# Layer 1's query, key and value projections as seven block products, with sums of the input streamed from DRAM

## The chip, the cores and the metric

The kernel runs on one core of a Trainium2 chip. The metric is the time of one execution on the device, in microseconds (us). A profile of one execution gives the records of TensorE (PE, with its weight loads as PEld), VectorE (DVE), ScalarE (ACT), GpSimd (POOL) and SyncE (SP, which issues the DMAs).

## The reference

The model is a two-layer encoder on 1024 tokens of width 1024, in float32. Layer 0 mixes tokens by neighbourhood attention, layer 1 by differential attention; each layer ends with a gated convolutional channel mixer and a gated embedding. The change touches layer 1's mixer only:

```python
def diff_attention(h, w_qkv, lam, subln_g, w_o, t5_table, lambda_init):
    q, k, v = jnp.split(h @ w_qkv, 3, axis=-1)      # 1024 x 3072
    # 8 heads; q and k of two 64-wide halves, q scaled by 1/8; v 128 wide
    ...
    def block_fn(args):                             # a block of 128 queries
        s = jnp.einsum('bhmqd,bhmkd->bhmqk', qb, k) + bias[None, :, None]
        a = jax.nn.softmax(s, axis=-1)
        w = a[:, :, 0] - lam_full * a[:, :, 1]
        return jnp.einsum('bhqk,bhkd->bhqd', w, v)
    ...
    o = rms_norm(o, subln_g) * (1.0 - lambda_init)
    return o @ w_o
```

`h` is the normalised input, `w_qkv` is 1024 x 3072, and the output o is 1024 x 1024.

## The kernel before

Every float32 operand of a projection is split into a high part, rounded by ACT to the type fp32r (`high`, L135), and a low part, the rest, by DVE (`low`, L138). A product is then three matmuls (`mm3`, L170): high by high, high by low, low by high. A block of 128 output columns by 512 tokens takes 8 slices of the inner width, so 24 matmuls of 128x512 into one PSUM bank; 128 columns by all 1024 tokens take 48. Layer 1's projections are 24 such column blocks: for each of 8 heads one of keys, one of queries, one of values, 1152 matmuls.

They run as a filler of the attention. `da` (L701) walks 64 steps n (8 heads of 8 query tiles). A step puts on PE, in this order, the values of tile n-1 (`da_values`, 8 matmuls), the scores of tile n+1 (`da_scores`, 12 matmuls), the first turn of tile n (`da_turn`, 4 transposes), some projection, the second turn, some projection, the small turn of tile n-1's output (`da_out`), and some projection. `tick` (L431) hands out the projection: it draws the generator `qkv_stream` (L323) forward, 6 draws of three matmuls in each step. `need` goes on drawing until the keys and queries, or the values, of a head are there. For each head the stream goes through keys, queries and values, with one weight block of 128 columns in use and the next being split. A finished bank of keys or queries is split into high and low on ACT and DVE; values are copied to SBUF, turned by PE and copied into `v` (L390).

Around a step, DVE adds the bias table T to the scores and takes a minimum (`softmax_pre`, L465), ACT takes the exponentials (L469), DVE combines the two softmaxes (L647 to L650), ACT and DVE copy the turned tile (L665, L667), ACT squares the values with a sum (L679), DVE adds a constant (L680), POOL takes the power -1/2 (`root`, L185), DVE scales the values (L682), and ACT copies their turn out (L698). T has one page for each head, loaded whole (L632).

The order on PE is the order of the program. A list scheduler sets the order on DVE, ACT, POOL and SP before the run; at run time each engine takes its instructions strictly in that order. Buffers come from rings of pages: `raw` holds three pages of 4 KB for each partition, `ws` four, `r1` and `r2` four larger ones each; projections have two PSUM banks (`pj`), turns and values two (`tr`), and scores the other four.

At the end of the stream come the embedding's product (`embeddings`, 96 matmuls), the output projection of the heads that are done (`first_out`), and the last head's (`second_out`).

## Time and profile before

| what | us |
|---|---|
| three runs | 2705.47, 2705.64 (median), 2705.91 |
| span of the profiled execution | 2703.4 |
| median of the runs less that span (the profiled execution's time is recorded as its span alone) | 2.2 |

By stage of the profiled execution (busy time of each engine, us; windows in us from the span's start):

| window | what runs | PE | DVE | ACT | POOL |
|---|---|---|---|---|---|
| 0 to 640 | layer 0, attention | 624.7 | 477.1 | 359.6 | 114.1 |
| 640 to 1010 | layer 0, channel mixer's first part | 368.9 | 278.9 | 154.8 | 114.1 |
| 1010 to 1285 | layer 0's end, layer 1's input | 275.0 | 191.5 | 132.8 | 21.7 |
| 1285 to 1330 | layer 1's first projections | 45.0 | 22.2 | 18.0 | 0.6 |
| 1330 to 1885 | layer 1's attention with its projections | 552.7 | 377.5 | 298.2 | 35.5 |
| 1885 to 2060 | the next stage | 172.9 | 141.2 | 87.0 | 21.8 |
| 2060 to 2703 | layer 1's rest | 636.6 | 449.8 | 269.8 | 129.8 |

The granted PE clock is 1.00 in all of these windows. An engine's busy time in a window is an upper bound of what it needs only where records do not overlap: PE's matmuls overlap, so their spacing is read from their starts. A row of the instructions in order of time gives start, duration, engine, line, operation, output<-inputs by the program's names and the shape; what stands in brackets at its end is how long the engine sat idle before it, and what ended that. A row of groups gives the count, the busy time and the mean in ns, and behind the second bar the idle time before the group with what ended it.

### The profile page before, as it was taken

The numbers are of one execution on the slowest core, as the hardware profiler recorded it, in microseconds if no ns is written. First come the engines' busy times: TensorE is split into PE (matmuls) and PEld (weight loads), VectorE is DVE, ScalarE is ACT, GpSimd is POOL, SyncE is SP. The second block draws the span as 40 slices with busy tenths as digits, with TensorE's granted clock in tenths as the row PEclk, the third lists the DMA queues.
The fourth block names the chain that finished last, engine by engine and source line by source line (L and its number), as shares of the span: only waits on it lengthen the run. The fifth ranks groups of instructions, "written<-read, shape, count | busy, mean of one in ns | idle before, by whom it ended". The sixth has DMA issues, their size and how long they took to land.

```text
span 2703.4 us, 36590 instructions
## 1 busy us (share of the span) xinstructions
PE 2675.6 (99%) x13492; PEld 2216.0 (82%) x13492; DVE 1938.2 (72%) x3334; ACT 1320.1 (49%) x2469; POOL 437.4 (16%) x445
## 2 busy tenths in 40 slices
PE   8999999999999999999999999999999999999999
PEld 6888887878888888888888888888878888888887
DVE  6777777699777767676566666676699777767674
ACT  5555556454344444454455555555454444444452
POOL 2221220003333300001000000000103334300000
PEclk9999999999999999999999999999999999999999
DMA  6213226423332373333211111123423232373442
GB/s 184 85 66 104 77 94 197 130 71 126 108 110 101 109 269 132 117 129 117 78 47 46 46 47 47 53 79 129 140 71 133 97 115 96 112 263 128 117 138 100
DMA packets 129334, 297.97 MB, mean 110 GB/s; under 512 B 11737, under 2 KB 37721, under 8 KB 129154
## 3 DMA queue, kind: packets, MB, share of 16 engines
q1 hardware_dynamic: 129154, 295.63, 33.1%
q8 instruction: 106, 1.74, 0.2%
q14 instruction: 74, 0.61, 0.1%
HBM read 221.17 MB, written 86.61 MB: 114 GB/s over the span
## 4 chain that ended last, share of the span: by engine, by line
PE 92%; DVE 4%; DMA 2%; ACT 2%; issue 1%; POOL 0%; SPq 0%; ACTq 0%; POOLq 0%; DVEq 0%
PE b L173 21%; PE b L174 21%; PE b L175 21%; PE g L830 6%; PE m L830 5%; PE b L676 4%; PE s L640 4%; PE b L662 2%; PE b L204 2%; PE b L830 2%; PE av L536 2%; PE b L509 1%; DMA x<-in_x 1%; PE s L490 1%; PE s L489 1%
## 5 line engine op out<-in xcount | busy, mean ns | idle before, releaser
L173 PE MATMUL b<-r,ws 128*128 128x512 f32 (+1 forms) x1344 | 547.0, 407 | 1.6 <-DVE r L308 1.6
L174 PE MATMUL b<-r,ws 128*128 128x512 f32 (+1 forms) x1344 | 519.6, 387 | 0.6 <-DVE r L139 0.4
L175 PE MATMUL b<-r,ws 128*128 128x512 f32 (+1 forms) x1344 | 519.1, 386 | 0.0
L175 PEld LDWEIGHTS b<-r,ws 128*128 128x128 f32 x1344 | 252.8, 188 | 53.1
L173 PEld LDWEIGHTS b<-r,ws 128*128 128x128 f32 x1344 | 253.4, 189 | 49.7 <-issue 3.3
L174 PEld LDWEIGHTS b<-r,ws 128*128 128x128 f32 x1344 | 254.2, 189 | 36.3 <-DVE r L139 1.9
L469 ACT ACTIVATE E<-E,mn 128x1024 f32<-128x1024 f32 (+2 forms) x256 | 221.5, 866 | 102.2 <-DVE mn L465 101.9
L173 PE MATMUL b<-r,r 128*128 128x512 f32 x680 | 268.8, 395 | 1.4 <-ACT ws L1571 1.0
L173 PE MATMUL b<-r,wa 128*128 128x512 f32 x688 | 268.0, 390 | 2.0 <-DVE B L1222 2.0
L175 PE MATMUL b<-r,wa 128*128 128x512 f32 x688 | 268.0, 389 | 0.0
L174 PE MATMUL b<-r,wa 128*128 128x512 f32 x688 | 267.7, 389 | 0.0
L174 PE MATMUL b<-r,r 128*128 128x512 f32 x680 | 265.2, 390 | 0.0
L175 PE MATMUL b<-r,r 128*128 128x512 f32 x680 | 265.0, 390 | 0.0
L185 POOL TENSOR_TENSOR ss<-ss,mhalf 128x1 f32<-128x1 f32 x128 | 74.9, 586 | 1093.5 <-DVE ss L680 560.2
L139 DVE TENSOR_TENSOR ws<-raw,ws 128x512 fp32r<-128x512 f32 (+3 forms) x168 | 167.8, 1005 | 53.4 <-ACT ws L136 51.9
L136 ACT ACTIVATE r<-raw 128x512 fp32r<-128x512 f32 (+1 forms) x168 | 110.6, 665 | 192.0 <-PE b L174 169.2
L136 ACT ACTIVATE ws<-raw 128x512 fp32r<-128x512 f32 (+3 forms) x168 | 124.5, 748 | 114.2 <-PE b L175 51.9
L139 DVE TENSOR_TENSOR r<-raw,r 128x512 fp32r<-128x512 f32 (+1 forms) x168 | 126.9, 760 | 68.4 <-ACT r L136 65.2
L830 PE MATMUL m<-r,ws 128*128 128x512 f32 x672 | 156.4, 391 | 0.0
L830 PE MATMUL g<-r,ws 128*128 128x512 f32 x672 | 155.8, 391 | 0.0
L465 DVE CUSTOM_DVE_ANT_0 E<-s,T 128x1024 f32<-128x1024 f32 x128 | 151.0, 1217 | 4.1 <-PE s L640 4.1
L173 PEld LDWEIGHTS b<-r,wa 128*128 128x128 f32 x688 | 129.2, 188 | 29.9 <-DVE B L1222 3.2
(188 smaller groups left out, 5072.5 us busy)
## 6 DMA issues: line engine op xcount, KB each, us to landing
raw<-in_w_in SPq DMA_DIRECT2D x86, 512.0 KB, 3.5
raw<-in_qkv SPq DMA_DIRECT2D x48, 512.0 KB, 5.6
spillS<-r SPq DMA_DIRECT2D x88, 256.0 KB, 3.0
r<-in_ffn_w_out SPq DMA_DIRECT2D x40, 512.0 KB, 6.0
raw<-spillS SPq DMA_DIRECT2D x40, 512.0 KB, 3.7
spillA<-B SPq DMA_DIRECT2D x66, 256.0 KB, 2.8
raw<-spillA SPq DMA_DIRECT2D x30, 512.0 KB, 3.9
x<-x SPq DMA_DIRECT2D x24, 512.0 KB, 3.6
```

The source lines that it names most:

```text
L136: return self.nc.scalar.activation(hi, src, AF.Copy).ins
L139: return self.nc.vector.tensor_tensor(out=lo, in0=src, in1=hi.bitcast(F32), op=ALU.subtract).ins
L173: mm(out, sta[0], mov[0], start=first, stop=False, skip_group_check=onto)
L174: mm(out, sta[0], mov[1], start=False, stop=False, skip_group_check=onto)
L175: mm(out, sta[1], mov[0], start=False, stop=last, skip_group_check=onto)
L185: self.nc.gpsimd.tensor_tensor(out=ss, in0=ss, in1=self.mhalf, op=ALU.pow)
L204: self.nc.tensor.transpose(t[:, k * P : k * P + P], h[:, c : c + P], self.ident)
L465: nc.vector.tensor_tensor_reduce(out=e, in0=s, in1=bias, scale=1.0, scalar=3e38, op0=ALU.add, op1=ALU.min, accum_out=mn)
L469: self.exp = nc.scalar.activation(e, e, AF.Exp, bias=mn, scale=-1.0, accum_out=sm).ins
L640: nc.tensor.matmul(s[m][:, w], A[o, a, q], A[o, b, w], start=z == 0, stop=z == 2)
L676: nc.tensor.matmul(o, wT[:, k], V[:, k], start=k == 0, stop=k == KT - 1)
L830: mm(out[half], a, b[:, w], start=first and k + z == 0, stop=last and k == n - 1 and z == 2)
```

## The change

The projections that come after the first head are done by a scheme of Strassen's kind. Take two column blocks of 128 (keys and queries of one head, or the values of two heads), the inner width in two halves and the tokens in two halves: weights and input are then 2 x 2 blocks A and B, and their product takes eight block products of 12 matmuls. The scheme takes seven, of sums of blocks. S1 to S4 are sums of weights, T1 to T4 sums of the input.

Four column blocks stay as they were (keys and queries of head 0, values of heads 0 and 1, 192 matmuls). The other 20 go in ten pairs of seven products of 12 matmuls, 840. So 1032 matmuls stand in place of 1152.

T1 to T4 serve all pairs and are made once, while the first projections run: POOL makes them from the split input (36 operations of 128x512), and ACT and DVE split the sums. T1 replaces block B12 of the input in SBUF; T2, T3 and T4 go to DRAM and are read back for every pair through a ring of four slots, 120 loads of 512 KB. S1 to S4 are made on POOL for each pair, and all seven weight operands are split on ACT and DVE for each pair. The products of a pair go into three banks, which two PSUM pages hold in turn; four of the seven results are added up on DVE, one on POOL, and copied on ACT. To make room, T, one of the two exponential pages, the turned tile wT, `os` and `ot` have one page in place of two; T is reloaded in pieces behind the last scores that use them. The embedding's operands use pages that the attention has left. `tick` draws 6.5 times a step for the first 16 steps and then 5.14 times.

```diff
+PAIRS = [("kq", 1), ("kq", 2), ("v", 2), ("kq", 3), ("kq", 4), ("v", 4), ("kq", 5), ("kq", 6), ("v", 6), ("kq", 7)]
+PRODUCTS = (
+    ("A11", "B11", 0), ("S2", "T2", 1), ("A12", "B21", 0), ("S3", "T3", 1), ("S1", "T1", 2), ("A22", "T4", 1), ("S4", "B22", 2),
+)
+class Pair:
...
+    def sums(self):
+        A, tt = self.A, self.trunk.nc.gpsimd.tensor_tensor
...
+        tt(out=A["S1"], in0=A["A21"], in1=A["A22"], op=ALU.add)
+        tt(out=A["S2"], in0=A["S1"], in1=A["A11"], op=ALU.subtract)
+        tt(out=A["S3"], in0=A["A11"], in1=A["A21"], op=ALU.subtract)
+        tt(out=A["S4"], in0=A["A12"], in1=A["S2"], op=ALU.subtract)
...
+    def put(self, a, turns, turn):
...
+        if a == "A11":
+            act(p1, ps[0], AF.Copy)
+        elif a == "S2":
+            tt(out=u, in0=ps[1], in1=p1, op=ALU.add)
...
+        elif a == "S3":
+            tt(out=w, in0=ps[1], in1=p1, op=ALU.add)
+        elif a == "S1":
+            act(c5, ps[2], AF.Copy)
+            nc.gpsimd.tensor_tensor(out=w, in0=w, in1=c5, op=ALU.add)
+            self.out(1, 1, w, turns, turn, 4)
+        elif a == "A22":
+            tt(out=p1, in0=ps[1], in1=p1, op=ALU.add)
+            self.out(1, 0, p1, turns, turn, 3)
+        else:
+            tt(out=u, in0=ps[2], in1=u, op=ALU.add)
+            self.out(0, 1, u, turns, turn, 3)
...
+    def da_stream(self, hT, x, first, mid):
...
+        def step():
+            for t in turns:
+                t[0] -= 1
+            if self.open and turns and turns[0][0] < 0:
+                turns.pop(0)[1]()
...
+        def sums(n):
...
+            if made:
+                for m, key, t in made.pop():
+                    self.split(t, ring[:, m % 4, 0], ring[:, m % 4, 1])
+                    nc.sync.dma_start(stash[key][m // 3], raw[:, m % 4])
...
+        def load(k):
+            if todo[k] < len(loads):
+                nc.sync.dma_start(raw[:, k], stash[loads[todo[k]]][k])
+                todo[k] += 1
...
+                for k in range(4):
+                    mov = (ring[:, k, 0], ring[:, k, 1]) if b in stash else tuple(o[:, k] for o in moving[b])
+                    o = p.o[a]
+                    self.mm3(ps, (o[:, 0, k], o[:, 1, k]), mov, first and k == 0, k == 3, not first)
+                    if b in stash:
+                        load(k)
+                    step()
+                    yield
+                p.put(a, turns, turn)
...
     def tick(self, part):
 
-        self.credit += part * 48 / 8
+        self.credit += part * self.rate
...
-            self.T = self.page(x, "T", (P, TW))
-            nc.sync.dma_start(self.T, self.skewed[h][:, P - 1 : P - 1 + TW])
+            self.T = self.page(x, "T", (P, TW), bufs=1)
+            self.load_T(0, 512, TW), self.load_T(0, 0, 512)
...
+        if h + 1 < D_HEADS:
+            for c0, c1 in {3: ((1408, TW),), 6: ((1024, 1408),), 7: ((512, 1024), (0, 512))}.get(t, ()):
+                self.load_T(h + 1, c0, c1)
...
+                self.rate = 6.5 if n < 2 * NT else 5.14
```

**First place: the start of the attention.** ACT before the change, from the exponentials of the first tiles over the first head's values to those of the third tile (`v` is the first head's values, `b` a PSUM bank, `os` the square of the values of step 1):

```order
L665 ACTIVATE wT_11365<-b_1585_11366 128x512
L469 ACTIVATE E_1577_11350,sum_11354<-E_1577_11350,mn_11352 128x1024
L469 ACTIVATE E_1578_11351,sum_11358<-E_1578_11351,mn_11356 128x1024
L136 ACTIVATE ws_11396<-raw_11394 128x1024
L403 ACTIVATE raw_11262<-b_1574_11320 128x512
L390 ACTIVATE v_11261<-b_1587_11387 128x512
L390 ACTIVATE v_11261<-b_1593_11423 128x512
L679 ACTIVATE os_11438,ss_11439<-b_1594_11429,sum_11287 128x128
L665 ACTIVATE wT_11473<-b_1607_11474 128x512
```

ACT at the same place in the changed kernel (`r_1550` holds the sums that POOL makes, `r_1549` is the ring's page, `r_1407` the input block that T1 replaces; L600 is the L403 of before, L590 the L390, L924 the L679, L910 the L665):

```order
L910 ACTIVATE wT_11406<-b_1584_11407 128x512
L708 ACTIVATE E_1576_11391,sum_11395<-E_1576_11391,mn_11393 128x1024
L708 ACTIVATE E_1577_11392,sum_11399<-E_1577_11392,mn_11397 128x1024
L600 ACTIVATE raw_11284<-b_1573_11350 128x512
L224 ACTIVATE r_1407_9843<-r_1550_11128 128x512
L590 ACTIVATE v_11283<-b_1592_11448 128x512
L224 ACTIVATE r_1407_9843<-r_1550_11128 128x512
L224 ACTIVATE r_1549_11127<-r_1550_11128 128x512
L224 ACTIVATE r_1407_9843<-r_1550_11128 128x512
L224 ACTIVATE r_1549_11127<-r_1550_11128 128x512
L224 ACTIVATE r_1407_9843<-r_1550_11128 128x512
L224 ACTIVATE r_1549_11127<-r_1550_11128 128x512
```

The next three are the second half of the first head's values, the square of step 1, and another split of a sum:

```order
L590 ACTIVATE v_11283<-b_1593_11480 128x512
L924 ACTIVATE os_11495,ss_11496<-b_1594_11486,sum_11310 128x128
L224 ACTIVATE r_1549_11127<-r_1550_11128 128x512
L910 ACTIVATE wT_11530<-b_1607_11531 128x512
L224 ACTIVATE r_1549_11127<-r_1550_11128 128x512
```

The two copies into `v` stood side by side; now six splits of sums stand between them, the last of them of the sum that is the 26th operation of POOL's row of sums. On POOL the first roots of the attention (`ss`) stood behind each other before:

```order
L185 TENSOR_TENSOR sx_11086<-sx_11086,mhalf 128x1
L185 TENSOR_TENSOR ss_11439<-ss_11439,mhalf 128x1
L185 TENSOR_TENSOR ss_11521<-ss_11521,mhalf 128x1
L185 TENSOR_TENSOR ss_11609<-ss_11609,mhalf 128x1
L185 TENSOR_TENSOR ss_11691<-ss_11691,mhalf 128x1
```

In the changed kernel the sums L560 to L570 begin behind `sx_11086`; the place shown is that of the first two roots (what stands ahead of these rows, up to `sx_11086`, is sums too; `raw_11558` and `raw_11560` are the first pair's weights):

```order
L568 TENSOR_TENSOR r_1550_11128<-r_1550_11128,r_1409_9845 128x512
L273 TENSOR_TENSOR ss_11496<-ss_11496,mhalf 128x1
L570 TENSOR_TENSOR r_1550_11128<-r_1550_11128,r_1410_9846 128x512
L567 TENSOR_TENSOR r_1550_11128<-r_1550_11128,r_1407_9843 128x512
L568 TENSOR_TENSOR r_1550_11128<-r_1550_11128,r_1409_9845 128x512
L118 TENSOR_TENSOR r_1550_11128<-raw_11560 128x512
L120 TENSOR_TENSOR r_1550_11128<-raw_11558,raw_11560 128x512
L569 TENSOR_TENSOR r_1550_11128<-r_1408_9844,r_1550_11128 128x512
L119 TENSOR_TENSOR r_1550_11128<-r_1550_11128,raw_11558 128x512
L273 TENSOR_TENSOR ss_11603<-ss_11603,mhalf 128x1
L570 TENSOR_TENSOR r_1550_11128<-r_1550_11128,r_1410_9846 128x512
```

The first root stands behind 31 sums, and between it and the second stand seven more, of the input and of the first pair's weights.

**Second place: DVE in one step of the second pair's time** (`s` the scores, `mn` the minimum's write-out, `c` and `sum` columns, `wT` the turned tile). Before:

```order
L465 ISA E_1990_13246,mn_13251<-s_13232,T_12629 128x1024
L465 ISA mn_13251 128x1
L667 COPY wT_13260<-b_1998_13273 128x512
L647 RECIPROCAL c_13255<-sum_13253 128x1
L648 SCALAR_TENSOR_TENSOR c_13255<-sum_13249,c_13255,neglam 128x1
L649 RECIPROCAL sum_13249<-sum_13249 128x1
L650 SCALAR_TENSOR_TENSOR E_1989_13245<-E_1990_13246,c_13255,E_1989_13245 128x1024
L680 TENSOR_SCALAR ss_13307<-ss_13307 128x1
L682 TENSOR_SCALAR os_13306<-b_2001_13297,sum_13159,ss_13307 128x128
```

The same step in the changed kernel (L704 is the L465 of before, L912 the L667, L892 to L895 the L647 to L650, L925 the L680; `r_1550` is the pair's working page, `ws` and `r_1884` the targets of splits):

```order
L704 ISA E_1951_13253,mn_13258<-s_13239,T_11289 128x1024
L704 ISA mn_13258 128x1
L912 COPY wT_13267<-b_1960_13292 128x512
L227 TENSOR_TENSOR ws_13285<-r_1550_11128,ws_13285 128x512
L172 TENSOR_TENSOR r_1550_11128<-b_1905_13020,r_1550_11128 128x512
L892 RECIPROCAL c_13262<-sum_13260 128x1
L893 SCALAR_TENSOR_TENSOR c_13262<-sum_13256,c_13262,neglam 128x1
L235 SCALAR_TENSOR_TENSOR r_1884_12934<-r_1550_11128,r_1884_12934 128x512
L894 RECIPROCAL sum_13256<-sum_13256 128x1
L895 SCALAR_TENSOR_TENSOR E_1950_13252<-E_1951_13253,c_13262,E_1950_13252 128x1024
L227 TENSOR_TENSOR ws_13368<-raw_13018,ws_13368 128x512
L235 SCALAR_TENSOR_TENSOR r_1884_12934<-r_1550_11128,r_1884_12934 128x512
```

Five operations of the pair stand in this step: two splits of weight operands (L227), a sum of block products (L172) and two splits of finished keys or queries (L235). A split and a sum stand ahead of L892, which waits for the exponentials.

More of the change, by code (lines that the diff above doesn't have):

```diff
@@ L641, in da_scores @@
         a = (NT - 1 - t) * P
-        e = [self.page(x, f"E{m}") for m in range(2)]
+        e = [self.page(x, f"E{m}", bufs=2 - m) for m in range(2)]
         r0, sm = [self.softmax_pre(s[m], self.T[:, a : a + SEQ], e[m]) for m in range(2)]
+        if h + 1 < D_HEADS:
+            for c0, c1 in {3: ((1408, TW),), 6: ((1024, 1408),), 7: ((512, 1024), (0, 512))}.get(t, ()):
+                self.load_T(h + 1, c0, c1)
         w = e[0]
@@ L656, in da_turn @@
         if g == 0:
-            self.chunk[n] = w, r0, self.page(x, "wT", (P, KT, P))
+            self.chunk[n] = w, r0, self.page(x, "wT", (P, KT, P), bufs=1)
         wT = self.chunk[n][2]
@@ L696, in da_out @@
         else:
-            ot = self.page(x, "ot", (P, P))
+            ot = self.page(x, "ot", (P, P), bufs=1)
             nc.scalar.activation(ot, tr, AF.Copy, scale=self.subg)
@@ L706, in da @@
         with self.tc.tile_pool(name="xa1", bufs=2, reuse_waits="tile") as x:
-            self.begin(self.qkv_stream(1, hT, x, first, mid))
+            self.begin(self.da_stream(hT, x, first, mid))
             self.chunk = {}
@@ L796, in last_rows @@
             self.part1 = None
-            self.jobs += [None, second]
+            self.jobs += [None] * 4 + [second]
     def job(self, act, dve):
@@ L1528, in embed, with embeddings @@
         yield hT, mid
-    def embeddings(self, layer):
+    def embeddings(self, layer, x=None):
         nc = self.nc
-        a = self.page(self.r2, "r2", (P, 2, 2, SEQ), F32R)
-        b = self.page(self.r2, "r2", (P, 2, 2, D), F32R)
+        late = lambda: (lambda o: [[o[:, k, z] for z in range(2)] for k in range(2)])(self.page(self.r2, "r2", (P, 2, 2, D), F32R))
+        a = b = None
+        if x is None:
+            a, b = late(), late()
+        else:
+            v = self.page(x, "v", (P, KT, P), bufs=3).bitcast(F32R).rearrange("p k n -> p (k n)")
+            w = [self.page(x, "proj", (P, D), F32R, bufs=3) for _ in range(3)]
+            a = [[v, w[0]], w[1:]]
         load = []
-        for o, src in ((a, self.i["pT"]), (b, self.i["ple_w_proj"])):
+        for to, src in ((lambda k: a[k], self.i["pT"]), (lambda k: b[k], self.i["ple_w_proj"])):
             for k in range(2):
-                load.append((src[layer][k * P : k * P + P], (o[:, k, 0], o[:, k, 1])))
+                load.append((src[layer][k * P : k * P + P], to, k))
         raws, done = [], []
@@ L1546, in job @@
         def job(n):
-            did = self.split(raws[n], *load[n][1])
+            did = self.split(raws[n], *load[n][1](load[n][2]))
             if len(raws) < len(load):
@@ L1555, in embeddings @@
         todo = [lambda n=n: job(n) for n in range(4)]
-        self.jobs += todo[: 2 if layer == 0 else 4]
+        self.jobs += todo[:2]
         self.after_values = [] if layer else todo[2:]
         yield
+        if x is not None:
+            b = late()
+            while len(done) < 2:
+                self.hurry()
+            begin(self.raw, "raw")
+            for w in (slice(0, 512), slice(512, D)):
+                for k in range(2):
+                    self.split(raws[2 + k][:, w], b[k][0][:, w], b[k][1][:, w])
+            done += [2, 3]
+            yield
         assert not self.after_values
```

171 lines of the change are left out of this document (165 added, 6 removed).

## Prediction

> **What bounds the kernel now.** I read the page first, then the busy time by stretches, then the instructions in order of time for one attention step, and last the groups by shape on POOL and DVE. The first line is the page's; the stretches cover layer 1's attention, where the change lies (columns: length, then busy time and count of PE, PEld, DVE, ACT, POOL, then granted clock, DMA share, GB/s).
>
> ```profile
> PE 2675.6 (99%) x13492; PEld 2216.0 (82%) x13492; DVE 1938.2 (72%) x3334; ACT 1320.1 (49%) x2469; POOL 437.4 (16%) x445
> 1330.00:1790.00 460.00, 460.00 (x2937) 379.30 (x2936) 309.40 (x621) 237.62 (x490) 29.12 (x53) 1.00 0.13 44
> 1790.00:1885.00 95.00, 92.70 (x574) 74.95 (x573) 68.12 (x128) 60.58 (x118) 6.36 (x10) 1.00 0.36 128
> ```
>
> PE is never idle from 1330 to 1790, at the full clock, while DVE is 67% busy, ACT 52%, POOL 6%. So PE sets the time here, and a matmul less is worth its slot on PE. Busy time does not give the slot, since matmuls overlap; the starts do (start, duration, engine and line):
>
> ```profile
> 1572.60 0.40 PE L174 MATMUL b<-r,ws 128*128 128x512 f32 x1
> 1572.84 0.39 PE L175 MATMUL b<-r,ws 128*128 128x512 f32 x1
> 1573.07 0.40 PE L173 MATMUL b<-r,ws 128*128 128x512 f32 x1
> 1573.30 0.39 PE L174 MATMUL b<-r,ws 128*128 128x512 f32 x1
> 1290.83 0.39 PE L175 MATMUL b<-r,ws 128*128 128x512 f32 x1
> 1294.68 0.39 PE L174 MATMUL b<-r,ws 128*128 128x512 f32 x1
> 1565.77 1.95 PE L676 MATMUL b<-v,wT 128*128 128x128 f32 x16
> 1567.65 1.66 PE L640 MATMUL s<-r 64*128 64x512 f32 x12
> 1574.44 1.95 PE L676 MATMUL b<-v,wT 128*128 128x128 f32 x16
> ```
>
> Each lasts 0.39 us, yet they start 0.70/3 = 0.23 us apart; over a longer run (the one that starts at 1290.83 and the seventeenth after it, at 1294.68: 3.85 us) it is 0.2265. I take 0.227. One step n of the attention (values, scores, two turns, 18 projection matmuls) lasts 1574.44 - 1565.77 = 8.67 us on PE.
>
> DVE works through the same step in a fixed order:
>
> ```profile
> 1569.19 0.41 DVE L682 TENSOR_SCALAR os<-b,sum,ss 128x128 f32<-128x128 f32 x1 [0.73 <-POOL ss L185]
> 1569.52 1.21 DVE L465 CUSTOM_DVE_ANT_0 E<-s,T 128x1024 f32<-128x1024 f32 x1
> 1571.80 0.69 DVE L667 COPY wT<-b 128x512 f32<-128x512 f32 x1
> 1573.25 0.17 DVE L647 RECIPROCAL c<-sum 128x1 f32<-128x1 f32 x1 [0.77 <-ACT E L469]
> 1573.79 1.26 DVE L650 SCALAR_TENSOR_TENSOR E<-E,c,E 128x1024 f32<-128x1024 f32 x1
> 1576.97 0.15 DVE L680 TENSOR_SCALAR ss<-ss 128x1 f32<-128x1 f32 x1 [1.92 <-ACT os L679]
> 1577.86 0.41 DVE L682 TENSOR_SCALAR os<-b,sum,ss 128x128 f32<-128x128 f32 x1 [0.73 <-POOL ss L185]
> ```
>
> From os to os is 8.67 us, of which 1.92 is spare (waiting for PE's values through ACT). So the bare DVE loop, with its waits for the exponentials (0.77) and for the root on POOL (0.73), is 6.75 us: this is the second bound, 1.92 us behind PE, and it holds no projection work in this step.
>
> **The change, part by part.** *Removed on PE.* Of 24 blocks of 48 matmuls (1152), four stay plain (192) and 20 become ten pairs of 7 x 12 = 84 (840): 1032. 120 matmuls go, 120 x 0.227 = **27.2 us** if nothing else becomes late. Scores, values and turns stay. A step holds 5.14 x 3 = 15.4 matmuls of projection instead of 18, so it shrinks to 8.67 - 2.6 x 0.227 = 8.08 us, and a pair spans 84/15.4 = 5.45 steps.
>
> *Added on DVE and ACT, steady part.* A key and query pair has on DVE seven operand splits, four block sums and four output splits, 15 operations of 128x512; two before (weights of 1024) plus four are replaced. Back to back such operations start 0.60 us apart:
>
> ```profile
> 2043.58 1.28 DVE L139 TENSOR_TENSOR wa<-r,wa 128x512 fp32r<-128x512 f32 x2
> ```
>
> 15 x 0.60 / 5.45 = 1.65 us a step. The wait of 0.77 for the exponentials takes in one of them in about half the steps (listing of the change, second place), 0.35. The loop is 6.75 + 1.65 - 0.35 = 8.05 us against PE's 8.08. A value pair has 11 operations: 7.6 us. ACT gains some ten half-size copies a pair, 6 us in 44, on top of 52% busy: hidden.
>
> *The shared resource.* The sums go to POOL, which was all but idle here. What POOL does to DVE is seen in layer 0's channel mixer:
>
> ```profile
> 760.32 1.29 POOL L1183 TENSOR_TENSOR r<-r,raw 128x512 f32<-128x512 f32 x1
> 760.42 1.74 DVE L139 TENSOR_TENSOR ws<-raw,ws 128x512 fp32r<-128x512 f32 x1
> 761.57 1.75 POOL L1225 TENSOR_TENSOR B<-B,c 128x512 f32<-128x512 f32 x1
> 762.47 0.69 DVE L1231 TENSOR_TENSOR u<-b,u 128x512 f32<-128x512 f32 x1 [0.32 <-PE b L175]
> L1183 POOL TENSOR_TENSOR r<-r,raw 128x512 f32<-128x512 f32 x17 | 23.2, 1363 | 1.2
> L1183 POOL TENSOR_TENSOR r<-raw,raw 128x512 f32<-128x512 f32 x17 | 22.9, 1347 | 155.7 <-DVE ws L139 150.1 <-DMA raw<-in_w_in 5.7
> L1183 POOL TENSOR_TENSOR r<-raw 128x512 f32<-128x512 f32 x17 | 22.8, 1340 | 39.2 <-DVE wa L139 20.0 <-DVE ws L139 19.2
> L1183 POOL TENSOR_TENSOR r<-raw,r 128x512 f32<-128x512 f32 x17 | 22.4, 1318 | 11.5 <-DVE wa L139 11.4
> L1225 POOL TENSOR_TENSOR B<-B,c 128x512 f32<-128x512 f32 x19 | 32.3, 1699 | 32.0 <-DVE B L1222 32.0
> ```
>
> The split that reads two SBUF tiles starts while POOL works and takes 1.74 us instead of 0.68: it ends 0.55 us after POOL's operation does; POOL's next is 0.46 longer. The sum that reads PSUM (u<-b,u) is not touched. The Trainium skill, SBUF — State Buffer, Who interferes with whom, says that the two share a port pair by an exclusive lock, so that the second to start blocks until the first is done; the row agrees, and the rule speaks against putting sums on POOL beside a loop with two-input operations.
>
> In the steady part POOL has five sums of 1.3 us a pair, 15% of its 44 us; a two-input DVE operation meets one with that chance and waits half of it, 0.1 us, about 2.8 times a step: 0.27 us. So the loop is 8.05 to 8.3 us against 8.08 in seven of ten pairs (38 steps). Least: nothing (PE still the longer one). Most: if every step were as full as the fullest that the listing shows (five projection operations: 6.75 - 0.77 + 5 x 0.60 = 8.98, 0.90 above PE's step; in 38 steps 34 us). I take the upper of the two means, 0.22 above PE's step, and with it 38 x 0.22 = 8.4, a little less since some of the meetings fall into a wait: **7 us**; ends 0 and 34.
>
> *The start.* Before the first pair, POOL makes T2, T3, T4 in 36 operations, and ACT and DVE split them. Queue order decides here (both listings of the first place). PE's first values need the second half of v, whose copy now stands on ACT behind the split of a sum that is POOL's 26th operation.
>
> ```profile
> 1295.78 0.60 ACT L136 ACTIVATE r<-b 128x512 fp32r<-128x512 f32 x1 [4.45 <-PE b L204]
> L390 ACT ACTIVATE v<-b x16: 584/594/598, 1325.4 to 1818.1; 128x512 f32<-128x512 f32 x16
> 1329.12 1.85 PE b L676 x16
> L136 ACT ACTIVATE wa<-r 128x512 fp32r<-128x512 f32 x130 | 81.3, 628 | 122.8 <-PE b L175 95.4 <-DVE r L1183 25.3 <-POOL r L1183 1.8
> ```
>
> POOL can begin when the last input tile is split, at 1296.4 (first row). PE would come to the values at 1329.1, or 0.7 earlier as it has three matmuls less ahead, and to their second half at 1329.4. With the bare 1.29 us, operation 26 ends at 1329.9, the split and the copy (0.63, 0.59) at 1331.1: PE waits 1.7 us. With 1.41, the mean of POOL's five groups of that shape in the mixer (1.32 to 1.70), it is 1334.3: 4.9 us. Then the root of the first step stands behind POOL's operation 31: 1340.7 with itself (0.55), os 0.4 later, and PE, at its small turn at 1339.9, waits 1.3; the second root, seven operations on, costs 1.0; the last sums go out to DRAM and back (3 to 4 us each way, row of spillS) before the first T products, 1.8. Together **9 us**. Ends: 2, and 20 if each of some twelve two-input operations of DVE holds POOL for its 0.6 to 1.2 us and waits for it in turn.
>
> *Elsewhere.* T, the bias table, has one buffer and is reloaded in pieces; the last comes after the last scores of a head and has 8.08 - 2.3 = 5.8 us:
>
> ```profile
> T<-t5s SPq DMA_DIRECT2D x8, 960.0 KB, 4.8
> raw<-spillS SPq DMA_DIRECT2D x40, 512.0 KB, 3.7
> spillS<-r SPq DMA_DIRECT2D x88, 256.0 KB, 3.0
> GB/s 184 85 66 104 77 94 197 130 71 126 108 110 101 109 269 132 117 129 117 78 47 46 46 47 47 53 79 129 140 71 133 97 115 96 112 263 128 117 138 100
> ```
>
> A quarter megabyte takes 3.0, and fits unless it queues behind the ring's loads (3.7 each); SP waits in order, so a ring load that waits for PE also holds oT's stores, and one buffer of ot then holds ACT. Ends 0 and 7 x 2; with the first scores of head 1, which follow their pair by three matmuls and the values, I take 2. The 120 ring loads are 63 MB in some 540 us, 117 GB/s beside the 44 to 128 of the rows above; the last of these rows (GB/s in 40 slices of the span) shows 269 in its busiest slice, so bandwidth holds. Embeddings and out-projection keep their matmuls; their added half splits are four of 0.6 us, beside 96 matmuls: nothing.
>
> **Sum.** Against the profiled execution's span: 2703.4 - 27.2 + 7 + 9 + 2 = 2694.2. The median of the runs (2705.6) lies 2.2 above the span, so **2696**: 0.35% faster, with two thirds of the gain given back.
>
> **Rivals.** (a) All is hidden: POOL near 1.29 a sum, loop under 8.08. For it: 1.92 us of spare DVE time in each step, and POOL's groups are mostly near 1.3. Against: the loop above has no margin left. 2703.4 - 27.2 + 2 + 2.2 = 2680, up to 2688.
> (b) The start costs its full 20 us, as POOL and DVE alternate while POOL never pauses: 2703.4 - 27.2 + 20 + 7 + 2 + 2.2 = 2707, no change. For it: the row of 1.74 us; against: POOL's groups in the mixer, with DVE as busy, stay at 1.3 to 1.4 in four of five. The rule of the Trainium skill, SBUF — State Buffer, Who interferes with whom, at full strength for each meeting, would give this time; the trace shows one such meeting, but not how often they fall here.
> (c) Slower: DVE becomes the bound of the pairs. At 8.98 us a step, 38 x 0.90 = 34 us: 2703.4 - 27.2 + 34 + 9 + 2 + 2.2 = 2723. It decides from (27.2 - 11)/38 = 0.43 above PE's step, a loop of 8.5. For it: two PSUM banks now turn over every 12 matmuls rather than 24, so that PE also waits for late sums; against: in the last row of stretches above DVE is 72% busy with whole splits and PE loses only 2.3 us of 95.
> (d) It doesn't take the matmuls out, or a plain path replaces them: the code yields 1032, so 2%.
>
> **How the numbers follow.** Forecast 0.35, (a) 0.17, (b) 0.24, (c) 0.22, (d) 0.02. 0.2% (5.4 us) is about what a measurement here can tell from no change: faster is below 2700, slower above 2711. Forecast and (a) are faster, but a part of the forecast's own range (2690 to 2704) is not: faster 0.49. Same: (b), (d) and that part, 0.28. Slower: (c) and a little of (b), 0.23. The range runs from inside (a) to inside (c): 2682 to 2714.
>
> **What would show it.** Right: 120 matmuls fewer; PE idle by 5 us near 1330, released by the copy of v on ACT, and again at the small turn by os; steps of 8.1 to 8.4 us later; operand splits on DVE of 0.68 with some of 1.2 to 1.8. (a): no PE wait above 2 us near 1330 and steps of 8.1. (b): a wait near 10 us there and POOL's sums at 1.6 or more. (c): steps of 8.6 and more in the pairs of keys and queries, and score, sum or split on DVE named as PE's releaser. Wrong altogether would be a wait for the ring's loads on PE, or a lower granted clock after the waits; I count neither.

## The result, and the profile after

| kernel | runs | median | range |
|---|---|---|---|
| before | 15 | 2705.40 us | 2704.56 to 2706.33 |
| changed | 15 | 2710.36 us | 2707.98 to 2715.42 |

The changed kernel is 0.2% slower: the ratio is 1.0020, with a 95% interval of 1.0012 to 1.0027. The time lies in the range of the prediction, but on the other side of the kernel before than was forecast. The 120 matmuls are gone (the page's count on PE falls from 13492 to 13372), and so 27 us of PE's work; all of it and 5 us more were lost again. The profiled execution has a span of 2706.7 us.

The page's engine line of the changed kernel (busy time, share, instructions):

```profile
PE 2660.8 (98%) x13372; PEld 2196.0 (81%) x13372; DVE 2021.1 (75%) x3442; ACT 1353.2 (50%) x2548; POOL 561.2 (21%) x531
```

Where it went is seen by stretches of time. First the kernel before (length, then busy time of PE, PEld, DVE, ACT, POOL with counts, granted clock, DMA share, GB/s), then the changed kernel:

```profile
1326.00:1364.00 38.00, 38.00 (x239) 31.38 (x238) 24.55 (x49) 17.90 (x37) 2.20 (x4) 1.00 0.07 22
1364.00:1800.00 436.00, 436.00 (x2786) 359.65 (x2785) 294.10 (x591) 226.66 (x465) 27.47 (x50) 1.00 0.14 47
```

```profile
1285.00:1326.00 41.00, 39.20 (x189) 30.97 (x187) 23.55 (x27) 14.96 (x24) 29.99 (x22) 1.00 0.25 89
1326.00:1364.00 38.00, 30.26 (x147) 23.45 (x148) 35.23 (x48) 21.58 (x44) 31.21 (x22) 0.82 0.55 201
1364.00:1800.00 436.00, 429.31 (x2739) 347.83 (x2737) 358.12 (x686) 256.08 (x534) 91.99 (x96) 1.00 0.59 197
```

Two losses, then. At the start PE is idle for 1.8 + 7.7 = 9.5 us, and from 1326 to 1364 the granted clock is 0.82 where it was 1.00; POOL is busy for 31 of 38 us. In the long steady stretch PE is idle for 6.7 us only, but its steps are longer than they need be. The values of steps 17 and 56 start here, before and after:

```profile
1469.45 2.01 PE L676 MATMUL b<-v,wT 128*128 128x128 f32 x16
1811.23 2.05 PE L676 MATMUL b<-v,wT 128*128 128x128 f32 x16
```

```profile
1493.36 1.95 PE L921 MATMUL b<-v,wT 128*128 128x128 f32 x16
1823.29 1.95 PE L921 MATMUL b<-v,wT 128*128 128x128 f32 x16
```

39 steps took 341.8 us before, 8.76 each, and take 329.9 now, 8.46 each. With 2.6 projection matmuls fewer a step (699 in this stretch before, 597 now) they should take 8.76 - 2.6 x 0.227 = 8.17. So 0.29 us a step is lost, 11 us in all, of which only a part shows as idle time, since a matmul's modelled end overlaps the next start. Who PE waited for from 1285 to 1885 (in total, times, longest):

```profile
PE b L907 <- ACT wT L910: 4.1, 3, 3.5
PE b L921 <- ACT v L590: 3.1, 2, 2.7
PE b L261 <- ACT ws L1835: 2.7, 1, 2.7
PE b L292 <- ACT wT L910: 2.4, 1, 2.4
PE b L935 <- DVE os L927: 1.9, 3, 1.1
PE b L921 <- DVE wT L912: 1.8, 4, 0.7
PE b L292 <- DVE wT L912: 1.7, 2, 1.3
PE s L882 <- DVE r L235: 0.6, 1, 0.6
PE s L882 <- DVE r L227: 0.5, 1, 0.5
```

The four on top are ACT's: copies of the turned tile, copies into v, and a copy of the embedding's product.

### The profile page after: what moved, and what is told of

Same layout as the page of the kernel before. It is cut to its first block, busy times and chain, and to the rows that moved or that the text cites. A ratio compares the mean times of both kernels' runs of the same rounds, so it can differ in the third digit from the quotient of the medians.

```text
span 2706.7 us, 37008 instructions
## 1 busy us (share of the span) xinstructions
PE 2660.8 (98%) x13372; PEld 2196.0 (81%) x13372; DVE 2021.1 (75%) x3442; ACT 1353.2 (50%) x2548; POOL 561.2 (21%) x531
## 4 chain that ended last, share of the span: by engine, by line
PE 38%; DVE 6%; ACT 2%; issue 2%; DMA 1%; POOL 1%; SPq 0%; ACTq 0%; DVEq 0%; POOLq 0%
PE b L261 9%; PE b L262 8%; PE b L263 8%; PE g L1078 3%; PE m L1078 3%; PE b L921 2%; PE s L882 2%; DVE E L704 1%; PE b L907 1%; DVE E L895 1%; ACT E L708 1%; PE b L1078 1%; PE b L292 1%; DVE ws L227 1%; DVE r L227 0%
## 5 line engine op out<-in xcount | busy, mean ns | idle before, releaser
L261 PE MATMUL b<-r,ws 128*128 128x512 f32 (+1 forms) x1304 | 532.3, 408 | 1.7 <-DVE r L396 1.6
L262 PE MATMUL b<-r,ws 128*128 128x512 f32 (+1 forms) x1304 | 505.2, 387 | 0.6 <-DVE r L227 0.5
L263 PE MATMUL b<-r,ws 128*128 128x512 f32 (+1 forms) x1304 | 505.6, 388 | 0.0
L263 PEld LDWEIGHTS b<-r,ws 128*128 128x128 f32 x1304 | 246.1, 189 | 51.3
L261 PEld LDWEIGHTS b<-r,ws 128*128 128x128 f32 x1304 | 247.4, 190 | 47.5 <-issue 3.5
L262 PEld LDWEIGHTS b<-r,ws 128*128 128x128 f32 x1304 | 247.9, 190 | 35.5 <-DVE r L227 1.9
L261 PE MATMUL b<-r,r 128*128 128x512 f32 x648 | 254.5, 393 | 0.9 <-ACT ws L1835 0.6
L262 PE MATMUL b<-r,r 128*128 128x512 f32 x648 | 252.7, 390 | 0.0
L263 PE MATMUL b<-r,r 128*128 128x512 f32 x648 | 252.5, 390 | 0.0
L227 DVE TENSOR_TENSOR ws<-raw,ws 128x512 fp32r<-128x512 f32 (+3 forms) x178 | 168.2, 951 | 46.4 <-ACT ws L224 44.2
L227 DVE TENSOR_TENSOR r<-raw,r 128x512 fp32r<-128x512 f32 (+1 forms) x168 | 124.4, 747 | 71.0 <-ACT r L224 67.7
L704 DVE CUSTOM_DVE_ANT_0 E<-s,T 128x1024 f32<-128x1024 f32 x128 | 151.1, 1217 | 1.7 <-PE s L882 1.7
```

The costliest lines, as they stand in the source:

```text
L227: return self.nc.vector.tensor_tensor(out=lo, in0=src, in1=hi.bitcast(F32), op=ALU.subtract).ins
L261: mm(out, sta[0], mov[0], start=first, stop=False, skip_group_check=onto)
L262: mm(out, sta[0], mov[1], start=False, stop=False, skip_group_check=onto)
L263: mm(out, sta[1], mov[0], start=False, stop=last, skip_group_check=onto)
L704: nc.vector.tensor_tensor_reduce(out=e, in0=s, in1=bias, scale=1.0, scalar=3e38, op0=ALU.add, op1=ALU.min, accum_out=mn)
```

## The experiments

Each kernel ran beside the kernel before on the same chip. Medians, and the ratio to the kernel before with its interval:

| run | us | ratio |
|---|---|---|
| e1_no_tsums | 2696.22 | 0.9966 (0.9953 to 0.9979) |
| e2_tsums_dve | 2703.51 | 0.9993 (0.9983 to 1.0002) |
| e3_no_pairsums | 2700.03 | 0.9980 (0.9971 to 0.9990) |
| e4_pairsums_dve | 2709.46 | 1.0014 (1.0004 to 1.0023) |
| e5_no_sums | 2685.71 | 0.9927 (0.9910 to 0.9943) |
| e6_spread | 2704.74 | 0.9997 (0.9988 to 1.0006) |
| e8_spread_dve | 2702.14 | 0.9989 (0.9980 to 0.9999) |
| e10_turn_act | 2718.85 | 1.0052 (1.0038 to 1.0065) |
| e11_all | 2713.33 | 1.0028 (1.0018 to 1.0038) |
| e14_best | 2701.55 | 0.9984 (0.9975 to 0.9993) |
| e15_no_lows | 2686.24 | 0.9925 (0.9910 to 0.9941) |
| e16_best2 | 2697.09 | 0.9967 (0.9955 to 0.9979) |
| e17_ticks | 2708.92 | 1.0014 (1.0005 to 1.0023) |
| e18_best_dve | 2692.15 | 0.9953 (0.9939 to 0.9966) |
| e9_waits (an edit of the kernel before; one run) | 2770.28 | |

### The start: POOL's sums

The chain of the first long wait, in order of time in the changed kernel (start, duration, what; in brackets the idle time before it and what ended it; other rows in between are left out):

```profile
1321.92 2.27 POOL L568 TENSOR_TENSOR r<-r,r 128x512 f32<-128x512 f32 x1
1324.22 0.63 ACT L224 ACTIVATE r<-r 128x512 fp32r<-128x512 f32 x1 [4.05 <-POOL r L568]
1325.45 0.63 ACT L224 ACTIVATE r<-r 128x512 fp32r<-128x512 f32 x1 [0.59 <-POOL r L570]
1325.98 0.58 ACT L910 ACTIVATE wT<-b 128x512 f32<-128x512 f32 x1
1326.61 0.66 PE L292 MATMUL b<-ident,raw 128*128 128x128 f32 x4 [2.37 <-ACT wT L910]
```

A sum on POOL ends, ACT splits it and the next one, and only then copies the turned tile out of its bank, which PE's next turn needs. ACT's splits of sums hold whatever copy stands behind them. The second wait (2.7 us, for the copy into v) has the same chain, behind the split of another sum. In the third and longest the split that holds the copy waits for something else, a store of an earlier sum that must leave the ring's slot:

```profile
1332.29 9.67 DVE L227 TENSOR_TENSOR r<-r,r 128x512 fp32r<-128x512 f32 x7
1345.00 0.63 ACT L224 ACTIVATE r<-r 128x512 fp32r<-128x512 f32 x1 [6.97 <-DMA stashT<-r]
1345.54 0.58 ACT L910 ACTIVATE wT<-b 128x512 f32<-128x512 f32 x1
1346.17 1.12 PE L907 MATMUL b<-ident,E 128*128 128x128 f32 x4 [3.54 <-ACT wT L910]
```

That store was issued at 1341.99, when VectorE had finished the low part, and landed at 1344.89. VectorE's seven splits before it took 1.38 us each, with POOL busy beside them, where such a split takes 0.69 without POOL's sums (below). Leaving out the sums tests all three; the splits, the stores and the loads stay, of unsummed data:

```diff
-                pool(out=t1, in0=b[1][0], in1=b[0][0], op=sub)
...
-                pool(out=t4, in0=t4, in1=b[2][1], op=add)
+            t2, t3, t4 = b[3][0], b[0][0], b[2][0]
```

> Left out: the 36 sums on POOL that make T1 to T4; the 16 splits on ACT and DVE, the stores and the 120 loads stay, of unsummed data, so the output is not the reference's. Theory A (the start's loss of about 16 us, 9.5 us of PE idle and 7 us at half clock before 1364, comes from POOL's sums, behind whose splits ACT's copies of the values stand): PE idle under 2 us between 1285 and 1364, no stretch of half clock, 2692 to 2697 us. Rival (the splits and the changed order alone hold PE, or the half clock comes from something else): over 5 us of idle there and 2703 us or more.

The kernel is 9.8 us faster than the one before and 14.1 below the changed one; from 1326 to 1364 (stretch as above) PE is busy again at the full clock:

```profile
1326.00:1364.00 38.00, 36.97 (x229) 29.99 (x229) 26.29 (x52) 23.35 (x48) 6.72 (x7) 1.00 0.30 91
```

So the start's loss, with its slow clock, comes from POOL's sums, directly or through what they delay; the splits and the changed order alone hold PE for 1 us. Next the same sums on VectorE:

```diff
-        tt, pool = nc.vector.tensor_tensor, nc.gpsimd.tensor_tensor
+        tt, pool = nc.vector.tensor_tensor, nc.vector.tensor_tensor
```

> The same 36 sums on VectorE instead of POOL. Theory A with the lock (a POOL sum takes 1.3 to 1.8 us and makes a two-input DVE operation beside it wait about 1 us): at 0.6 to 0.7 us a sum the sums take 24 us of DVE, are done some 20 us sooner, and the start loses 8 us rather than 16: 2700 to 2705 us. Rival (DVE is full there and the sums push every step): the start loses more than with POOL, 2712 us or more.

2703.5, as expected: the start loses 7.4 us of PE's time to waits rather than 9.5, with one stretch of half clock rather than several.

### The steady part: POOL's sums

```diff
-        tt(out=A["S1"], in0=A["A21"], in1=A["A22"], op=ALU.add)
...
+        A["S1"], A["S2"], A["S3"], A["S4"] = A["A21"], A["A11"], A["A21"], A["A12"]
...
-            nc.gpsimd.tensor_tensor(out=w, in0=w, in1=c5, op=ALU.add)
```

> Left out: POOL's five sums of each pair (S1 to S4 and one sum of products); the splits take unsummed weights, so the output is not the reference's. Theory B (the steady loss of some 14 us between 1364 and 1800 comes half from POOL holding two-input DVE operations, 0.38 us a step by their means): splits of 0.69 us and combines of 1.26 throughout, steps 0.2 to 0.3 us shorter, 2698 to 2704 us. Theory C (DVE's own added splits and sums overfill single steps, POOL matters little): 2706 to 2710 us.

The time is 10 us below the changed kernel, and 39 steps take 323.0 us (8.28 each) in place of 329.9. Groups on VectorE from 1364 to 1800 (count, busy time, mean in ns, idle before), first the changed kernel, then this one:

```profile
L895 DVE SCALAR_TENSOR_TENSOR E<-E,c,E 128x1024 f32<-128x1024 f32 x50 | 69.2, 1385 | 0.0
L227 DVE TENSOR_TENSOR ws<-r,ws 128x512 fp32r<-128x512 f32 x39 | 33.1, 848 | 4.1 <-ACT ws L224 4.1
L893 DVE SCALAR_TENSOR_TENSOR c<-sum,c,neglam 128x1 f32<-128x1 f32 x50 | 17.2, 344 | 1.6
```

```profile
L890 DVE SCALAR_TENSOR_TENSOR E<-E,c,E 128x1024 f32<-128x1024 f32 x51 | 64.6, 1267 | 0.0
L222 DVE TENSOR_TENSOR ws<-raw,ws 128x512 fp32r<-128x512 f32 x66 | 45.2, 686 | 4.6 <-ACT ws L219 4.6
L888 DVE SCALAR_TENSOR_TENSOR c<-sum,c,neglam 128x1 f32<-128x1 f32 x51 | 11.2, 219 | 1.6
```

The combine, the split and even the operation on a column of 128 numbers are longer while POOL sums: 0.12, 0.16 and 0.12 us on average. (The split reads unsummed weights in this run; in e4 below, where it reads sums that VectorE made, it takes 684 ns too.) The column's operation lasts 0.22 us without POOL's sums, so the rest of its 0.34 is waiting.

POOL's sums can delay a step in a second way, by late results. VectorE waits for the root on POOL for 40.6 us in this stretch of the changed kernel, at most 1.9 at once, and for 35.8, at most 1.0, in e3; ACT waits 7.5 us for the sum of products on POOL, and no longer in e3. Neither this run nor e18 separates the two ways: both runs take away both.

Both edits, e1's and e3's, at once:

> Both left out, all of POOL's sums (output not the reference's). If the two losses are separate, the gains of the two runs before add up; by A and B together 2683 to 2691 us; by A and C 2690 to 2695 us. What is then left of the 27 us that the 120 matmuls are worth is lost to DVE and ACT work alone.

2685.7, 20.3 us below the kernel before. The two gains (14.1 and 10.3) add up to 24.4; together they are 24.7. They are separate.

Then the same five sums on VectorE:

```diff
-        A, tt = self.A, self.trunk.nc.gpsimd.tensor_tensor
+        A, tt = self.A, self.trunk.nc.vector.tensor_tensor
...
-            nc.gpsimd.tensor_tensor(out=w, in0=w, in1=c5, op=ALU.add)
+            nc.vector.tensor_tensor(out=w, in0=w, in1=c5, op=ALU.add)
```

> The five sums of each pair on VectorE instead of POOL, all else as in the changed kernel. They add 5 x 0.69 us = 3.4 us of DVE a pair, 0.63 us a step, and take away the waits of DVE's two-input operations for POOL, 0.38 us a step by their means. If the lock costs PE as much as DVE's own time does, the steady part gets 0.2 us a step longer, some 10 us in all but for what falls into waits: 2711 to 2719 us. If a wait for POOL hits worse places than a sum that the order knows of, 2703 to 2708 us.

2709.5 lies between the two cases and settles neither: the steady steps were shorter (325.9 us in 39), but the first pair's sums made the crowded start worse, with 13.2 us of idle time there, though with two windows at half clock in place of four. e18 below takes the start out of the comparison.

### Not VectorE's amount of work

The prediction took the steady loss for VectorE running out of time. Three runs speak against that. One moves a copy of 0.69 us a step from VectorE to ACT:

```diff
-            self.job(self.turned_w, nc.vector.tensor_copy(wT[:, 4:8], t).ins)
+            if 8 <= n < 55:
+                self.turned_w = nc.scalar.activation(wT[:, 4:8], t, AF.Copy).ins
...
```

> The changed kernel with the copy of the second turn made on ScalarE instead of VectorE in steps 8 to 54: 0.69 us less DVE in each step, 0.6 us more ACT. If DVE is the bound of the steady part (steps 0.35 us over PE's), that loss goes: PE idle between 1364 and 1800 falls from 6.7 to under 2 us and the time by 8 to 13 us, to 2697 to 2703 us. If the loss is single late results behind POOL (the root behind a sum) or late banks, or ACT now is late with the copy: 2707 us or more.

It made things worse, by some 8 us against the changed kernel. 39 steps take 337.0 us, 7.1 more; in that lies one window at half clock, which costs 1.7, and a second one follows the embedding's wait. The changed kernel's profile has neither. VectorE's waits for the exponentials from 1420 to 1800 in this run:

```profile
DVE c L892 <- ACT E L708: 36.8, 33, 1.8
```

In the changed kernel they were 14.3 us from 1364 to 1800. The copy stands on ACT among the exponentials that VectorE's combine waits for: a step is also a chain through both engines, and this run lengthened ACT's part of it. By itself it does not show that VectorE had time to spare. Another run leaves out all of POOL's sums and also VectorE's splits for the weights' low parts (the third is e18, below):

```diff
-        self.o[k] = self.trunk.operand(self.A[k])
+        o = t.page(t.ws, "ws", (P, 2, 4, P), F32R)
+        t.high(self.A[k], o[:, 0])
```

> All of POOL's sums left out as before, and in the pairs also VectorE's seven splits for the low part of the weight operands (the high part is used in its place; output not the reference's): 7 x 0.69 us in 5.45 steps, 0.9 us of DVE a step. If what is left without the sums (7 us between the 2685.7 there and the 27 us below the kernel before) is the chain of a step through DVE and ACT, that goes: 2678 to 2682 us. If it is something else (banks, transfers): 2684 us or more.

2686.2, the same as e5 (2685.7): VectorE's busy time from 1364 to 1800 falls from 349.5 to 312.4 us and nothing is gained. What is lost without POOL's sums (steps of 8.28 against 8.17) is not VectorE's amount of work.

A part of it could be in PE's own order. At 5.14 draws a step, eleven of the 48 steps between 1420 and 1830 have one draw between the two turns, not two, and PE then starts the second turn 0.43 to 0.46 us after the last matmul's start, not 0.23, as ACT's copy of the first turn isn't done yet (here it ends at 1803.06):

```profile
1802.66 0.40 PE L263 MATMUL b<-r,ws 128*128 128x512 f32 x1
1803.12 0.66 PE L907 MATMUL b<-ident,E 128*128 128x128 f32 x4
```

```diff
-                self.tick(0.34)
+                self.tick(0.4)
...
-                self.tick(0.16)
+                self.tick(0.1)
```

> The changed kernel with that last edit alone. In ten of fifty steps it has one draw (three matmuls) between the turns, and PE starts the second turn 0.44 us after the last matmul there instead of 0.23. If that is a term of the steady loss: 1 to 3 us below the changed kernel, 2707 to 2709.5 us, and no 0.44 us left. If PE's place in a step matters little, or the small turn, now closer behind the second turn, waits instead: 2710 us or more.

No such gap is left, but the time, 2708.9, cannot be told from that of the changed kernel (their ratios' intervals overlap), and the steps are 8.43 against 8.46. That term is 1 us at most, and the rest of the 0.11 us a step stays open.

### A start that is spread

The sums for T1 to T4 need not crowd three steps. If head 1's keys and queries stay plain (12 matmuls more, 2.7 us), ten blocks of projection lie ahead of the first pair, and the sums can be ordered behind the attention's own operations:

```diff
-PAIRS = [("kq", 1), ("kq", 2), ("v", 2), ...
+PAIRS = [("kq", 2), ("v", 2), ...
...
+        def pool(**k):
+            self.behind([nc.gpsimd.tensor_tensor(**k).ins], [self.rooted])
```

> Keys and queries of head 1 go plain too (nine pairs, 12 matmuls more, 2.7 us), so that the sums on POOL can spread over ten blocks; each group of sums is put behind the attention's roots that come before it in the program, and T1's splits come three blocks later. Theory A: the start's loss falls from 16 to under 5 us, no half clock, and one pair's steady loss (1.4 us) goes too: 2698 to 2704 us, faster than the kernel before. Rival (POOL at any density holds DVE, and DVE holds PE): over 8 us are still lost before 1400, 2706 us or more.

2704.7, in neither case: the start lost 4.4 us of idle time in place of 9.5, but one wait of 3.0 us for ACT's copy of the values still halved the clock. With the sums on VectorE, each group behind the last combine:

```diff
-            self.behind([nc.gpsimd.tensor_tensor(**k).ins], [self.rooted])
+            self.behind([tt(**k).ins], self.paced)
```

> The same spread, with the sums that make T1 to T4 on VectorE, each group behind the combine of the step before it. 36 x 0.69 = 25 us of DVE over some twelve steps, 2.0 us a step beside 1.9 spare. With no lock there: 2697 to 2703 us, level with the spread on POOL or a little better. Rival (DVE's steps overflow): 5 us or more worse than the spread on POOL.

2702.1: level or a little better, as expected. What was left of the start's waits was one of 2.6 us, where the last of these sums, T1's splits and the first pair's sums on POOL met: the root that PE's small turn needed could start at 1362.4 and started at 1366.4, behind three of POOL's sums, the first of which took 3.48 us. Then three edits at once, the sums one block sooner, e10's move of the copy, and

```diff
-                nc.scalar.activation(e[:, w], o, AF.Copy)
+                if half and x is not None:
+                    nc.vector.tensor_copy(e[:, w], o)
```

> The spread start on VectorE with its sums one block sooner, the second turn's copy on ScalarE in steps 8 to 54, and every second copy of the embedding's product on VectorE. If the losses are separate: 2702 us less 8 to 13 for the copy, 2 to 4 for the start's last wait with its half clock, 2 for the embedding: 2684 to 2691 us, faster than both kernels by over 0.5%. If they stand behind each other (a wait that goes gives way to the next): 2693 us or more.

2713.3, 11 us worse than e8: it holds e10's move of the copy, which cost 8 us alone. Without that, with T1's splits spread too, the first pair's sums behind the root that comes before them and the embedding's copies all on VectorE:

```diff
+        def late(kt):
+            if kt % 2 == 0:
+                k = kt // 2
+                self.behind(self.split(room[:, k], B12[0][:, k], B12[1][:, k]), self.paced)
```

> The spread start with the sums for T1 to T4 on VectorE, one block sooner, T1's four splits one in two draws behind a combine, the first pair's sums on POOL behind the root that comes before them, and both copies of the embedding's banks on VectorE; the second turn's copy stays on VectorE. If the start's losses are the crowding of single steps: under 2 us idle before 1420, no half clock, 2694 to 2699 us, faster than both kernels. If they move on instead: 2701 us or more. The embedding's wait of 2.7 us: under 1 us if ACT's queue made it, unchanged if not.

2701.6, above the first range. The start was cured (PE's waits from 1285 to 1420: 2.1 us in all, full clock), but the embedding's copies were better off on ACT. On VectorE PE waited 4.4 us for them, 4.1 of these at once, where it had been 2.7:

```profile
PE b L267 <- DVE ws L1862: 4.4, 2, 4.1
```

Two windows at half clock followed that wait; one follows the shorter wait in e16, the next run.

With them back on ACT, and e17's edit:

> The spread start as in the run before, the embedding's copies back on ScalarE, and the projection between the two turns of a step always at least two draws (the parts of a step 0.4, 0.1 and 0.5 in place of 0.34, 0.16 and 0.5). If the embedding's wait and its half clock held the run before back, and the short stretches between turns cost 2 us: 2693 to 2698 us. If the waits only move: 2700 us or more.

2697.1, faster than both kernels. Last, the sums of the later pairs on VectorE, now that the start is free of them:

```diff
-            did = self.trunk.nc.gpsimd.tensor_tensor(**k).ins
+            did = (self.trunk.nc.vector if after is None else self.trunk.nc.gpsimd).tensor_tensor(**k).ins
...
-            nc.gpsimd.tensor_tensor(out=w, in0=w, in1=c5, op=ALU.add)
+            nc.vector.tensor_tensor(out=w, in0=w, in1=c5, op=ALU.add)
```

> The run before with the spread start, and the five sums of each later pair on VectorE; the first pair's four stay on POOL. With the sums on VectorE alone the steady steps were 8.36 us against 8.46 (329.9 to 325.9 us in 39 steps), while the whole stayed level, since the first pair's sums crowded the start. If a sum on POOL costs a steady step more than the same sum on VectorE, though it takes 3.4 us of VectorE a pair: 2692 to 2695 us, steps of 8.35. If the earlier difference in the steps came from where that start left the order: 2697 us or more, steps of 8.45.

2692.2, 0.47% faster than the kernel before (0.34 to 0.61%). 39 steps take 324.0 us in place of 329.8 in e16, though VectorE is busier (371.5 us from 1364 to 1800 against 362.5): a sum on POOL costs a step more than the same sum on VectorE. The combine shows one reason; it took 1366 ns in e16, and nothing holds it now:

```profile
L920 DVE SCALAR_TENSOR_TENSOR E<-E,c,E 128x1024 f32<-128x1024 f32 x51 | 64.5, 1265 | 0.0
```

Late results are the other: the longest of VectorE's waits for a root falls from 1.9 to 0.7 us, and PE's two waits for `os`, 2.4 us in e16, to 1.5.

### The clock

To see whether waits of PE alone lower the granted clock, ACT's copy of the turned tile is repeated in five steps of the kernel before:

```diff
-            self.turned_w = nc.scalar.activation(wT[:, 0:4], t, AF.Copy).ins
+            for _ in range({20: 10, 28: 12, 36: 14, 44: 17, 52: 21}.get(n, 1)):
+                self.turned_w = nc.scalar.activation(wT[:, 0:4], t, AF.Copy).ins
```

> The kernel before, with ACT's copy of the turned tile made 10, 12, 14, 17 and 21 times over at steps 20, 28, 36, 44 and 52 (same values), so that PE waits in five places of an attention that has no wait: about 0 to 1, 1 to 2, 2 to 3, 4 to 5 and 6 to 8 us. If waits of 2 us and more make the clock drop, there are stretches of half clock of 3.4 us or a multiple behind the last three and none behind the first, and matmuls 0.43 us apart in them; how much of a window of 3.4 us must be idle shows from where the waits lie. If the half clock in the changed kernel came from something else (POOL's load, the transfers), there is none here.

The waits came out longer than meant, 7.3 to 14.2 us, because PE's second turn already waits for the copy of the first. So this run has no short wait to show where the drop begins; it does show that waits alone, in the kernel before with an idle POOL, halve the clock. Cut into windows of 3.41 us, around the first of the five waits (columns as above):

```profile
1500.06:1503.47 3.41, 1.74 (x10) 1.13 (x7) 2.33 (x5) 2.73 (x5) 0.00 (x0) 1.00 0.00 0
1503.47:1506.89 3.42, 0.00 (x0) 0.00 (x0) 1.73 (x4) 3.29 (x7) 0.00 (x0) 1.00 0.00 0
1506.89:1510.30 3.41, 1.17 (x5) 1.18 (x6) 0.02 (x1) 2.09 (x4) 0.00 (x0) 0.50 0.03 5
1510.30:1513.71 3.41, 3.41 (x10) 2.53 (x10) 0.67 (x1) 0.37 (x1) 0.00 (x0) 0.50 0.06 19
1513.71:1517.13 3.42, 3.42 (x27) 3.02 (x27) 0.00 (x0) 0.45 (x2) 0.00 (x0) 1.00 0.00 0
```

## Why the prediction was wrong

**Right:** 120 matmuls went; the start's mechanism (ACT's copies behind splits of POOL's sums) in two of its three long waits; the ring's loads are hidden (no wait of PE for them in the list above), though the ring's stores are not (the third wait of the start); T's reload costs PE nothing that shows there, and the first scores of head 1 wait 0.6 us and 0.5 for splits on VectorE, of 2 us predicted for both.

That the start's idle time came out so close, 9 us predicted and 9.5 measured, is partly luck: of its terms the copy of v was put at 4.9 and came to 2.7, the root and `os` were put at 2.3 and came to 0.2, and two waits for copies of the turned tile, 5.9 us, were not among them.

**The step that failed is the start's price, "or a lower granted clock after the waits; I count neither".** The three long waits of the start, 2.4, 2.7 and 3.5 us, are each followed by half clock. The granted clock in the changed kernel, in windows of 3.41 us:

```profile
1324.08:1327.50 3.42, 1.05 (x7) 0.85 (x7) 2.62 (x4) 2.10 (x4) 3.42 (x4) 1.00 0.22 89
1327.50:1330.91 3.41, 3.41 (x10) 2.63 (x9) 3.22 (x8) 3.41 (x7) 3.41 (x3) 0.50 0.51 211
1330.91:1334.32 3.41, 2.72 (x18) 2.22 (x17) 3.41 (x3) 2.76 (x6) 3.33 (x3) 1.00 0.03 11
1334.32:1337.74 3.42, 1.37 (x10) 1.25 (x12) 3.42 (x3) 1.29 (x3) 2.79 (x3) 1.00 0.00 0
1337.74:1341.15 3.41, 3.41 (x17) 2.38 (x16) 3.41 (x3) 0.29 (x2) 3.07 (x2) 0.50 0.56 229
1341.15:1344.56 3.41, 1.48 (x7) 0.88 (x5) 3.16 (x7) 0.00 (x0) 2.52 (x3) 1.00 0.77 251
1344.56:1347.98 3.42, 1.81 (x7) 1.62 (x8) 2.32 (x4) 2.98 (x6) 1.87 (x3) 0.50 0.89 322
1347.98:1351.39 3.41, 3.41 (x10) 2.63 (x9) 2.29 (x5) 3.21 (x7) 3.33 (x3) 0.50 0.74 292
```

In the four windows at 0.50 PE is busy for 3.41 + 3.41 + 1.81 + 3.41 = 12.0 us and does half of what it could: 6 us lost. With 9.5 of idle time the start costs 15.5, not 9; e1, without the sums, gets 14.1 of it back.

**The steady term was mis-sized:** 7 us predicted, 11 measured in 39 steps. Its working mixed a right cause with a wrong one. POOL's hold on VectorE was put at 0.27 us a step; POOL's sums, by their hold and their late results together, cost PE 6.9 us in 39 steps by e3, 0.18 a step. The other part, VectorE's count of operations against PE's step, is no bound here: seven operations fewer a pair gained nothing (e15), five more gave 5 us when they replaced POOL's (e18). What a step obeys is more likely the chain of scores, minimum, exponential and combine through two engines in a fixed order; e10 fits that, but no run shows it by itself, and 0.11 us a step stays open.

**"Nothing" for the embedding** was short by 1.7 us: PE waits 2.7 for ACT's copy there; in the kernel before these waits come to 1.0:

```profile
PE b L830 <- ACT ws L1571: 0.6, 1, 0.6
PE b L173 <- ACT ws L1571: 0.4, 2, 0.3
```

Together: -27.2 + 15.5 + 11 + 1.7, and 3 for steps 3 to 16 (1363.22 to 1485.12, 9.38 us each, where 1.6 matmuls more than before ask for 8.76 + 0.36) make +4.0; the spans say +3.3. The sum of the prediction had no term for these early steps. The clock alone would not have turned its sign: 2696 + 6 is 2702, still below the kernel before; with the 4 us by which the steady term was short it is 2706. Of the rivals, (b), a start of 20 us, comes nearest in its time, 2707; its cause (POOL and VectorE alternating) is a part only, as POOL's sums averaged 1.3 to 1.8 us there, and over a third of the start's cost is the clock's.

## What to carry to other kernels

A wait of PE is to be priced with the clock that it leaves behind: here a wait of 2.4 us and more that fell into one window of 3.41 us cost half of the next window or two as well. Work for an idle engine is not free if an in-order engine must read its result ahead of something that PE waits for: look at what stands behind the reader, and spread the producer or move it, which here, with both done and twelve matmuls put back, turned +0.2% into -0.5%. And before work is moved to balance two engines, look at the chain through both, not only at their busy time: moving 0.69 us a step to the less busy one cost 8 us here, of which its profile puts 3.4 down to the clock.
